# Small matmuls of two heads on two halves of the TensorE array, in fewer and larger groups

## The chip, the core and the metric

The kernel runs on one core of a Trainium2 chip. A core has a 128x128 matmul array (TensorE, in the profile PE, with its weight loads as PEld), VectorE (DVE), ScalarE (ACT), GpSimd (POOL) and SyncE (SP), which here issues the DMAs. Each engine runs its own instructions in order and waits on semaphores for the others. The metric is the device time of one execution in microseconds; lower is better.

## What is computed

One layer of a hybrid decoder on a prompt of 2048 rows and on 8 sequences of 4 new rows, all in fp32, width 1024. The input is normalised and multiplied by one wide matrix. One branch is a short gated convolution, the other an RWKV-7 time mixing with 16 heads of 64; both are projected, gated, added, and projected once more. The part that this change is about is the recurrence of the second branch:

```python
def step(S, inp):
    r_t, k_t, v_t, d_t, kk_t, a_t = inp
    sa = jnp.einsum('bhvk,bhk->bhv', S, -kk_t)
    S = (S * d_t[:, :, None, :] + sa[..., None] * (kk_t * a_t)[:, :, None, :]
         + v_t[..., None] * k_t[:, :, None, :])
    y = jnp.einsum('bhvk,bhk->bhv', S, r_t)
    return S, y
```

S is a 64x64 state per head. It runs over 2048 rows for the prompt and over 4 rows, from a given state, for each of the 8 sequences.

## The kernel before

**Sets, pairs, chunks.** The prompt is cut in 4 sets of 512 rows; the last set carries the 32 sample rows too. The 16 heads go as 8 pairs, one head on partitions 0 to 63 and the other on 64 to 127 (`HS[0]`, `HS[1]`). In each set and pair the recurrence is done in 8 chunks (`NCH`) of 64 rows, so 32 pairs of 8 chunks in all; the samples of a pair are a ninth chunk (index `NCH`) in the last set.

**The steps of a pair** are generators, each a "side":
- `rwkv_keys` makes the scaled keys and queries AR and BK, `[128, chunk, 2, 64]`.
- `rwkv_solve` forms the *scores* (lines 904 to 917): for each chunk and head a matmul of BK by AR over the 64 partitions of that head, four chunks to a group. Head 0 goes to one PSUM tile `pt`, head 1 to another, and DVE masks each into GM. Then it inverts small triangular blocks.
- `rwkv_merge` composes the inverse Xbd with 32x32 matmuls, which are issued head by head in turn (lines 962 to 965).
- `rwkv_load` writes the values of the chunks into `SV[64:128]`.
- `rwkv_chain` (lines 1051 to 1093) runs the chunks in order. Per chunk: a matmul of AR by the state S into `pa`; two DVE additions (one a head) of `pa` and P1 into `us`; `inner`, a matmul of Xbd by `us`, copied into `SV[0:64]` by DVE and ACT; a matmul of BKt by SV; two DVE instructions that make the new S. Those are three links that return to PE: `us`, SV and S.
- `own_values` (1023 to 1032) makes P1 = G K V, what the chunk's own values give: for each chunk and head a 64x64 matmul of GM by `SV[64:128]`, both heads into PSUM partitions 0 to 63, and an ACT copy into P1. It is called for two chunks at a time: once ahead of the chain and three times inside it.
- `own_rows` (1040 to 1049) adds the chunks' own part to the output rows Yc, four chunks to a group: one matmul a chunk with both heads' GM as 128 columns by both heads' SV, which fills four 64x64 blocks of which two are used; two DVE additions pick them. It runs behind the fourth and the eighth chunk.
- `rwkv_sequences` does the same for the samples with w = 1, and `rwkv_out` normalises Yc and stores it.

**What sets the order.** The main stream is projections of 24 passes to a block (`proj`, PSUM tile `ip`), which PE could run without a pause. While the program is built, `drive` goes along the main stream and lets the live sides issue steps between its matmuls. A planner, class `Clock`, keeps a reckoned time of each engine from `Traced.cost`. A side yields the tiles that its next step reads, and is not continued before `clock.t["PE"]` has reached the time at which these are reckoned to be ready, nor before its share of the main stream has come. So the order on each engine is fixed when the program is built, and the costs in `Traced.cost` decide it. The sides of a pair spread over the main stream of a pair; the chain of one pair runs beside keys, solve and merge of the next. Behind the last pair no main stream is left, and what remains of its sides is issued by `finish_sides` (line 1365).

**PSUM.** `pt` has two buffers that all steps but the chain's `pa` and `pb` share.

All instructions are recorded under line 98, the helper, so the profile is read by tile names.

Of the kernel before, what the change touches and what calls it, by code (L numbers as in the profile page):

```python
# [7 lines left out]
F32 = mybir.dt.float32  # L8
# [3 lines left out]
ALU = mybir.AluOpType  # L12
# [4 lines left out]
P = 128  # L17
# [4 lines left out]
NCH = 8  # L22
# [4 lines left out]
W = {"sq": 1.0, "norm": 1.0, "lora": 2.0, "one": 1.0, "scan": 2.0, "exp": 2.0, "key": 1.0, "bones": 1.5,  # L27
     "sv": 1.5, "bt": 2.0, "score": 4.0, "inv0": 5.0, "inv": 0.45, "inv1": 4.0, "merge": 2.0,
     "gk": 1.3, "us": 1.3, "sa": 1.3, "state": 1.3, "samp": 2.0, "gn": 4.0, "out": 2.0}
# [8 lines left out]
class Clock:  # L38
# [3 lines left out]
    def __init__(self):  # L42
        self.t = dict.fromkeys(("PE", "DVE", "ACT", "POOL", "SP"), 0.0)
        self.log = {}
        self.held = {"DVE": [], "POOL": []}

    @staticmethod
# [40 lines left out]
class Traced:  # L88
# [18 lines left out]
    def cost(self, op, out, ins, k):  # L107
        n = out.free_size()
        if self.name == "PE":
            if op == "transpose":  # L110
                return 109.0
            lhs, rhs = k["lhsT"], k["rhs"]
            if rhs.dtype == F32R:
                return 8 + 0.45 * n
            return 2 * max(0.84 * max(lhs.free_size(), n), 26.0)
        if self.name == "DVE":
            per = {"transpose": 1.6, "tensor_tensor_scan": 2.1}.get(op, 1.05)
            if op == "tensor_reduce":
                n = ins[0].free_size()
            return 170 + per * n  # L120
        if self.name == "ACT":
            return 200 + 0.84 * n + 90 * max(0, len(ins) - 1)
        if k.get("op") == ALU.pow:
            return 1650.0
        return 120 + 2.3 * n if op == "tensor_tensor" else 120 + 1.0 * n
# [26 lines left out]
def hybrid_kernel(tc, x_prompt, x_sample, state_conv, state_shift, state_rwkv, norm_g, w_in, conv_w,  # L152
# [220 lines left out]
    rw = ph1.enter_context(tc.tile_pool(name="rw", bufs=1))  # L373
# [15 lines left out]
    SV = xp.tile([P, NC1, P], F32, name="SV")  # L389
# [507 lines left out]
    def rwkv_solve(th, p, o):  # L897

        AR = o["AR"]
        samp = th == LAST  # L900
        GM = GMB[(th * NB + p) % 2]


        for c0 in range(0, NCH + samp, 4):
            cs = range(c0, min(NCH + samp, c0 + 4))
            pp = [ps_t.tile([P, 512], F32, name="pt") for _ in range(2)]
            for h in range(2):
                for c in cs:
                    T.matmul(pp[h][:, (c - c0) * P:(c - c0 + 1) * P], lhsT=BK[HS[h], c].rearrange("p q t -> p (q t)"),
                             rhs=AR[HS[h], c].rearrange("p q t -> p (q t)"), start=True, stop=True)  # L910
            k = len(cs)
            mk = mask_s if c0 == NCH else mask_p
            for h in range(2):
                V.tensor_tensor(out=GM[:, c0:c0 + k, :, h, :],
                                in0=pp[h][:, 0:k * P].rearrange("p (c a t) -> p c a t", a=2, t=64),
                                in1=mk.unsqueeze(1).broadcast_to([P, k, 2, 64]), op=ALU.mult)
            yield W["score"]


        Mc = rw.tile([P, NCH, 32], F32, name="Mc")  # L920
        for i, g in enumerate(blk):
            h, b = i // 2, slice(i % 2 * 32, i % 2 * 32 + 32)
            A.copy(Mc[g], GM[b, 0:NCH, 0, h, b])
        yield 0.5, [Mc]
        Mi = rw.tile([P, 32, 32], F32, name="Mi")
        V.transpose(Mi.rearrange("p t (e c) -> p t e c", c=NCH),
                    Mc.rearrange("p c t -> p t c").unsqueeze(2).broadcast_to([P, 32, 4, NCH]))
        X = rw.tile([P, 8, 32], F32, name="X")
        A.copy(X, X0)
        Mo = rw.tile([P, NCH, 32], F32, name="Mo")  # L930
        A.copy(Mo[64:96], GM[0:32, 0:NCH, 0, 1, 32:64])
        yield W["inv0"], [Mi, X]

        for j in range(31, 0, -1):
            c0 = j // 4
            tt = sm.tile([P, 80], F32, name="tt")
            tv = tt[:, 0:(8 - c0) * j].rearrange("p (c i) -> p c i", i=j)
            V.tensor_tensor(out=tv, in0=Mi[:, j, 0:j].unsqueeze(1).broadcast_to([P, 8 - c0, j]),
                            in1=X[:, c0:8, j:j + 1].broadcast_to([P, 8 - c0, j]), op=ALU.mult)
            V.tensor_tensor(out=X[:, c0:8, 0:j], in0=X[:, c0:8, 0:j], in1=tv, op=ALU.add)  # L940
            yield W["inv"]
        Xo = rw.tile([P, 8, 4, 8], F32, name="Xo")
        V.transpose(Xo.rearrange("p a e c -> p (a e c)"), X.rearrange("p a b -> p (a b)"))
        o.update(GM=GM, Xo=Xo, Mo=Mo)
        yield W["inv"]
# [77 lines left out]
    def own_values(c0, w, GM):  # L1023

        pt = ps_t.tile([P, 512], F32, name="pt")
        for i in range(w):
            for h in range(2):
                T.matmul(pt[0:64, i * P + h * 64:i * P + (h + 1) * 64], lhsT=GM[64:128, c0 + i, 0, h, :],
                         rhs=SV[64:128, c0 + i, HS[h]], start=True, stop=True)
        P1 = sm.tile([64, 2, P], F32, name="P1")  # L1030
        A.copy(P1[:, 0:w, :], pt[0:64, 0:w * P].rearrange("p (c x) -> p c x", x=P))
        return P1

    def inner(c, pb, us, Xbd):

# [4 lines left out]
    def own_rows(c0, w, GM, Yc):  # L1040

        pt = ps_t.tile([P, 512], F32, name="pt")
        for i in range(w):
            T.matmul(pt[:, i * P:(i + 1) * P], lhsT=GM[:, c0 + i, 1].rearrange("p h t -> p (h t)"), rhs=SV[:, c0 + i, :],
                     start=True, stop=True)
        for h in range(2):
            V.tensor_tensor(out=Yc[HS[h], c0:c0 + w, :],
                            in0=pt[HS[h], 0:w * P].rearrange("p (c x) -> p c x", x=P)[:, :, HS[h]],
                            in1=Yc[HS[h], c0:c0 + w, :], op=ALU.add)

    def rwkv_chain(th, p, o):

        Yc = y_tile(th, o)
        AR, pe, GM, Xbd = (o[k] for k in ("AR", "pe", "GM", "Xbd"))
        samp = th == LAST
        S = St[p]

        nxt = own_values(0, 2, GM)
        yield W["gk"], [nxt]
        for g in range(0, NCH, 4):  # L1060
            pa = ps_a.tile([P, 4, P], F32, name="pa")
            for c in range(g, g + 4):
                PC = pe[:, c:c + 1]
                T.matmul(pa[:, c - g, :], lhsT=AR[:, c].rearrange("p q t -> p (q t)"), rhs=S, start=True, stop=True)
                if c % 2 == 0:
                    P1 = nxt
                us = sm.tile([P, 64], F32, name="us")
                for h in range(2):
                    V.tensor_tensor(out=us[HS[h]], in0=pa[0:64, c - g, HS[h]], in1=P1[:, c % 2, HS[h]], op=ALU.add)
                sp = sm.tile([P, P], F32, name="sp")  # L1070
                A.activation(out=sp, in_=S, func=AF.Copy, scale=PC)
                yield W["us"], [us]
                pb = ps_b.tile([P, 2, P], F32, name="pb")
                inner(c, pb[:, 0], us, Xbd)
                yield W["sa"], [SV[0:64, c, :]]
                T.matmul(pb[:, 1, :], lhsT=BKt[:, c, :], rhs=SV[:, c, :], start=True, stop=True)
                for h in range(2):
                    V.scalar_tensor_tensor(out=S[HS[h], HS[h]], in0=pb[HS[h], 1, HS[h]], scalar=PC[HS[h]], in1=sp[HS[h], HS[h]],
                                           op0=ALU.mult, op1=ALU.add)
                if c % 2 == 0 and c + 2 < NCH:  # L1080
                    nxt = own_values(c + 2, 2, GM)
                yield W["state"], [S]
            for h in range(2):
                A.copy(Yc[HS[h], g:g + 4, :], pa[64:128, :, HS[h]])
            yield W["out"], [SV[0:64, g:g + 4]]
            own_rows(g, 4, GM, Yc)
        if samp:
            pt = ps_t.tile([P, 512], F32, name="pt")
            T.transpose(pt[:, 0:P], S, ident)
            so = sm.tile([P, P], F32, name="sq")  # L1090
            V.tensor_copy(so, pt[:, 0:P])
            for h in range(2):
                SP.dma_start(out=new_rwkv_p[0, 0, 2 * p + h], in_=so[HS[h], HS[h]])

    def rwkv_sequences(th, p, o):
# [22 lines left out]
            V.tensor_reduce(out=UY[:, HS[h]], in_=ms.rearrange("p j v -> p v j"), axis=AX.X, op=ALU.add)  # L1118
            A.copy(Yc[HS[h], c, :], UY[64:128, HS[h]])
        us = sm.tile([P, 64], F32, name="us2", bufs=1)  # L1120
        P1 = own_values(c, 1, GM)
        for h in range(2):
            V.tensor_tensor(out=us[HS[h]], in0=UY[0:64, HS[h]], in1=P1[:, 0, HS[h]], op=ALU.add)
        yield W["samp"], [us]
        inner(c, ps_t.tile([P, 512], F32, name="pt"), us, o["Xbd"])
        mss = []
# [364 lines left out]
```

## Time and profile before

| | |
|---|---|
| median of 3 runs | 3385.74 us (3383.95 to 3388.24) |
| the profiled execution | 3391.1 us |
| its span, first to last instruction | 3389.4 us |
| granted TensorE clock, mean | 0.982 |
| instructions | 54068 |
| DMA | 606.60 MB, mean 179 GB/s |

The span is what the profile's windows and timeline run over; the execution takes 1.7 us more. An instruction is written `out<-in`, by tile names without buffer numbers, with rows*columns of the array that a matmul uses: 64*64 is a quarter of it. In the group view the numbers behind the bar are the busy time of the group in us, the mean ns of one, and the idle time of the engine ahead of it with what ended it. In the timeline each row has start and length in us; the end of a matmul record lies some 0.2 us behind the moment at which the array takes the next, so rows overlap, and steps are read from start to start or from end to end.

### The profile page before, as it was taken

What the parts mean: (1) busy time and instruction counts of PE and PEld (TensorE: products, weight loads), DVE (VectorE), ACT (ScalarE), POOL (GpSimd) and SP (SyncE); (2) the same over time, 40 slices, a digit from 0 to 9 for tenths busy, and PEclk for the clock granted to TensorE, in tenths of its full rate; (3) what the DMA queues carried; (4) which work ended last, traced back from release to release, by engine and by line L of the source; (5) the groups of instructions that cost most, each with busy time, mean ns of one, the idle gap of its engine ahead of it and who ended that gap; (6) DMA issues with size and microseconds to landing.
All of it is one profiled execution on the core that took longest, in us unless ns stands there. A gap on an engine that the chain in (4) does not pass through costs nothing.

```text
span 3389.4 us, 54068 instructions
## 1 busy us (share of the span) xinstructions
PE 3257.8 (96%) x20706; PEld 2722.5 (80%) x20706; DVE 2039.6 (60%) x5815; ACT 1265.2 (37%) x2660; POOL 300.2 (9%) x517
## 2 busy tenths in 40 slices
PE   7999999999999999999999999999999997999998
PEld 6777777877777778777777898888888885878897
DVE  5676777766666557555666666677666645433332
ACT  5444444443334443344333344334333332211101
POOL 2110000110001011010001010001000000000000
PEclk9999999999999999999999999999999997999999
DMA  8786666544444444444444443334333347989773
GB/s 278 247 270 209 202 215 214 181 136 137 148 156 146 144 152 167 141 153 140 149 150 150 138 152 116 128 111 135 134 124 105 110 156 243 342 314 324 265 247 130
DMA packets 233305, 606.60 MB, mean 179 GB/s; under 512 B 32906, under 2 KB 136451, under 8 KB 179286
## 3 DMA queue, kind: packets, MB, share of 16 engines
q1 hardware_dynamic: 232902, 602.61, 52.6%
q8 instruction: 164, 2.69, 0.3%
q14 instruction: 95, 0.78, 0.1%
q0 software_dynamic: 144, 0.52, 0.0%
HBM read 447.90 MB, written 155.17 MB: 178 GB/s over the span
## 4 chain that ended last, share of the span: by engine, by line
PE 71%; DVE 16%; issue 5%; ACT 5%; DMA 1%; POOL 1%; DVEq 0%; ACTq 0%; SPq 0%; POOLq 0%
PE ip L98 50%; PE pt L98 12%; PE po L98 5%; DVE X L98 3%; PE pb L98 3%; DVE tt L98 3%; ACT tmp L98 2%; DVE tmp L98 2%; DVE Mi L98 1%; PE pa L98 1%; DVE us L98 1%; DVE whl L98 1%; DVE S L98 1%; ACT Xbd L98 1%; ACT Mc L98 1%
## 5 line engine op out<-in xcount | busy, mean ns | idle before, releaser
L98 PE MATMUL ip<-XH,whl 128*128 128x512 f32 (+3 forms) x7408 | 2053.5, 358 | 6.8 <-ACT whl L98 2.6
L98 PEld LDWEIGHTS ip<-XH,whl 128*128 128x128 f32 x7408 | 1281.9, 191 | 166.8 <-issue 12.8
L98 PE MATMUL ip<-XL,whl 128*128 128x512 f32 (+3 forms) x3704 | 1313.7, 355 | 3.3 <-POOL XL L98 3.3
L98 PEld LDWEIGHTS ip<-XL,whl 128*128 128x128 f32 x3704 | 706.1, 191 | 94.0 <-issue 11.7
L98 DVE TENSOR_TENSOR X<-X,tt 128x60 f32<-128x60 f32 (+24 forms) x992 | 214.5, 216 | 29.4
L98 DVE TENSOR_TENSOR tt<-Mi,X 128x60 f32<-128x60 f32 (+24 forms) x992 | 210.5, 212 | 29.1
L98 DVE SCALAR_TENSOR_TENSOR S<-pb,pe,sp 64x64 f32<-64x64 f32 x512 | 143.4, 280 | 75.9 <-PE pb L98 69.6
L98 ACT COPY SV<-pb 64x64 f32<-64x64 f32 x256 | 53.3, 208 | 362.7 <-DVE SV L98 360.4
L98 PEld LDWEIGHTS pt<-SV,GM 64*64 64x64 f32 (+1 forms) x1584 | 142.5, 155 | 49.1 <-DVE tmp L98 14.5
L98 ACT ACTIVATE tmp<-ip,vec 128x512 f32<-128x512 f32 (+2 forms) x174 | 102.8, 592 | 198.6 <-PE ip L98 196.2
L98 PE MATMUL pt<-SV,GM 64*64 64x64 f32 (+1 forms) x1584 | 167.4, 244 | 9.5 <-DVE tmp L98 7.6
L98 PE MATMUL ip<-RH,whl 128*128 128x512 f32 (+2 forms) x640 | 170.5, 355 | 5.6 <-ACT RH L98 5.6
L98 ACT ACTIVATE sp<-S,pe 128x128 f32<-128x128 f32 x256 | 99.5, 400 | 196.7 <-DVE S L98 194.3
L98 PE MATMUL po<-whl,MH 128*128 128x512 f32 x544 | 170.3, 394 | 0.0
L98 DVE TENSOR_TENSOR us<-pa,P 64x64 f32<-64x64 f32 x512 | 110.6, 216 | 86.3 <-PE pa L98 78.2
L98 DVE TENSOR_TENSOR whl<-wraw,whl 128x1024 fp32r<-128x1024 f32 x105 | 130.2, 1241 | 48.6 <-ACT whl L98 46.6
L98 DVE SCALAR_TENSOR_TENSOR gt<-gt,ip 128x512 f32<-128x512 f32 (+1 forms) x80 | 47.0, 587 | 167.1 <-PE ip L98 164.0
L98 ACT CAST whl<-wraw 128x1024 fp32r<-128x1024 f32 x105 | 109.5, 1043 | 80.4 <-DMA wraw<-in_w_o_dram 20.1
L98 PE MATMUL pt<-AR,BK 64*128 64x128 f32 x1056 | 129.1, 287 | 3.7 <-DVE GM L98 3.7
L98 PEld LDWEIGHTS ip<-RH,whl 128*128 128x128 f32 x640 | 112.7, 189 | 24.6 <-issue 4.0
L98 PEld LDWEIGHTS pb<-us,Xbd 128*128 128x128 f32 x512 | 87.6, 190 | 55.6 <-DVE us L98 18.7
L98 PEld LDWEIGHTS pt<-AR,BK 64*128 64x128 f32 x1056 | 112.2, 188 | 24.6 <-DVE GM L98 8.2
(487 smaller groups left out, 4085.5 us busy)
## 6 DMA issues: line engine op xcount, KB each, us to landing
wraw<-in_w_in_dram SPq DMA_DIRECT2D x81, 512.0 KB
whl<-w_k SPq DMA_DIRECT2D x24, 1024.0 KB
whl<-w_r SPq DMA_DIRECT2D x24, 1024.0 KB
whl<-w_v SPq DMA_DIRECT2D x24, 1024.0 KB
whl<-w_z SPq DMA_DIRECT2D x24, 1024.0 KB
whl<-w_xin SPq DMA_DIRECT2D x24, 1024.0 KB
whl<-w_cg SPq DMA_DIRECT2D x24, 1024.0 KB
whl<-w_zc SPq DMA_DIRECT2D x24, 1024.0 KB
```

The costliest lines, as they stand in the source:

```text
L98: r = f(*a, **k)
```

## The change

Three places issue their matmuls in another way, and the planner reckons narrow matmuls anew.

- Scores: within a group the two heads alternate chunk by chunk, where one head's four came before the other's.
- `own_values`: head 1 writes PSUM partitions 64 to 127, where both wrote 0 to 63, and it is called once for all 8 chunks ahead of the chain. One ACT copy `[128, 512]` makes P1; the calls inside the chain are gone. For the samples DVE reads PSUM directly, with no copy.
- `own_rows`: one matmul a head and chunk, 64 columns wide, head 0 on PSUM partitions 0 to 63 and head 1 on 64 to 127; called once for all 8 chunks behind the chain, with one DVE addition `[128, 512]`.
- `Traced.cost`: an fp32 matmul that uses part of the array costs its time divided by 1.9, and each change of the array's form costs 170 ns.

```diff
+        self.mode = (128, 128)
...
             if rhs.dtype == F32R:
-                return 8 + 0.45 * n
-            return 2 * max(0.84 * max(lhs.free_size(), n), 26.0)
+                mode, t = (P, P), 8 + 0.45 * n
+            else:
+                part = [next(x for x in (32, 64, 128) if v <= x) for v in (lhs.ap[0][1], lhs.free_size())]
+                mode, t = tuple(part), 2 * max(0.84 * max(lhs.free_size(), n), 26.0) / (1 if part == [P, P] else 1.9)
+            t += 170 * (mode != self.clock.mode)
+            self.clock.mode = mode
+            return t
...
-            for h in range(2):
-                for c in cs:
+            for c in cs:
+                for h in range(2):
                     T.matmul(pp[h][:, (c - c0) * P:(c - c0 + 1) * P], lhsT=BK[HS[h], c].rearrange("p q t -> p (q t)"),
                              rhs=AR[HS[h], c].rearrange("p q t -> p (q t)"), start=True, stop=True)
...
         for i in range(w):
             for h in range(2):
-                T.matmul(pt[0:64, i * P + h * 64:i * P + (h + 1) * 64], lhsT=GM[64:128, c0 + i, 0, h, :],
-                         rhs=SV[64:128, c0 + i, HS[h]], start=True, stop=True)
-        P1 = sm.tile([64, 2, P], F32, name="P1")
-        A.copy(P1[:, 0:w, :], pt[0:64, 0:w * P].rearrange("p (c x) -> p c x", x=P))
-        return P1
+                T.matmul(pt[HS[h], i * 64:(i + 1) * 64], lhsT=GM[64:128, c0 + i, 0, h, :], rhs=SV[64:128, c0 + i, HS[h]],
+                         start=True, stop=True)
+        return pt
...
         for i in range(w):
-            T.matmul(pt[:, i * P:(i + 1) * P], lhsT=GM[:, c0 + i, 1].rearrange("p h t -> p (h t)"), rhs=SV[:, c0 + i, :],
-                     start=True, stop=True)
-        for h in range(2):
-            V.tensor_tensor(out=Yc[HS[h], c0:c0 + w, :],
-                            in0=pt[HS[h], 0:w * P].rearrange("p (c x) -> p c x", x=P)[:, :, HS[h]],
-                            in1=Yc[HS[h], c0:c0 + w, :], op=ALU.add)
+            for h in range(2):
+                T.matmul(pt[HS[h], i * 64:(i + 1) * 64], lhsT=GM[:, c0 + i, 1, h, :], rhs=SV[:, c0 + i, HS[h]],
+                         start=True, stop=True)
+        Y = Yc[:, c0:c0 + w, :].rearrange("p c v -> p (c v)")
+        V.tensor_tensor(out=Y, in0=pt[:, 0:w * 64], in1=Y, op=ALU.add)
...
-        nxt = own_values(0, 2, GM)
-        yield W["gk"], [nxt]
+        P1 = rw.tile([P, NCH, 64], F32, name="P1")
+        A.copy(P1.rearrange("p c v -> p (c v)"), own_values(0, NCH, GM))
+        yield W["gk"], [P1]
...
-                if c % 2 == 0:
-                    P1 = nxt
                 us = sm.tile([P, 64], F32, name="us")
                 for h in range(2):
-                    V.tensor_tensor(out=us[HS[h]], in0=pa[0:64, c - g, HS[h]], in1=P1[:, c % 2, HS[h]], op=ALU.add)
+                    V.tensor_tensor(out=us[HS[h]], in0=pa[0:64, c - g, HS[h]], in1=P1[HS[h], c, :], op=ALU.add)
...
-                if c % 2 == 0 and c + 2 < NCH:
-                    nxt = own_values(c + 2, 2, GM)
                 yield W["state"], [S]
...
-            yield W["out"], [SV[0:64, g:g + 4]]
-            own_rows(g, 4, GM, Yc)
+        yield W["out"], [SV[0:64, 0:NCH]]
+        own_rows(0, NCH, GM, Yc)
```

More of the change, by code (lines that the diff above doesn't have):

```diff
@@ L1120, in rwkv_sequences @@
         us = sm.tile([P, 64], F32, name="us2", bufs=1)
-        P1 = own_values(c, 1, GM)
+        pt = own_values(c, 1, GM)
         for h in range(2):
-            V.tensor_tensor(out=us[HS[h]], in0=UY[0:64, HS[h]], in1=P1[:, 0, HS[h]], op=ALU.add)
+            V.tensor_tensor(out=us[HS[h]], in0=UY[0:64, HS[h]], in1=pt[HS[h], 0:64], op=ALU.add)
         yield W["samp"], [us]
```

## The prediction

> **What bounds the kernel now.** I read four views, from coarse to fine. First the page: busy shares, the 40 slices and the chain of work that ended last.
>
> ```profile
> PE 3257.8 (96%) x20706; PEld 2722.5 (80%) x20706; DVE 2039.6 (60%) x5815; ACT 1265.2 (37%) x2660; POOL 300.2 (9%) x517
> PE   7999999999999999999999999999999997999998
> PE 71%; DVE 16%; issue 5%; ACT 5%; DMA 1%; POOL 1%; DVEq 0%; ACTq 0%; SPq 0%; POOLq 0%
> ```
>
> PE is full in all slices but the first, one late and the last, and the chain is mostly PE. A share over the whole span hides stages, so the windows come next: us, then busy us of PE, PEld, DVE, ACT, POOL, clock, DMA share, GB/s.
>
> ```profile
> 84.00:2700.00 2616.00, 2543.90 (x16945) 2122.20 (x16944) 1713.57 (x5133) 1081.55 (x2315) 254.99 (x432) 0.99 0.47 157
> 2780.00:2850.00 70.00, 47.06 (x182) 31.32 (x182) 42.14 (x81) 22.02 (x41) 5.57 (x4) 0.73 0.59 195
> 2850.00:3389.00 539.00, 524.33 (x2608) 441.19 (x2606) 193.74 (x371) 89.43 (x170) 11.43 (x17) 0.99 0.76 273
> ```
>
> In the first row, the stage where all changed code runs, PE is busy 97% and DVE 65.5% (1713.57 of 2616). The second row is the tail of that stage, where one chain of short steps is bare; the third is the merge and output stage, which the change does not touch. What PE waits for, in us, times and the longest, tells what other links are near it:
>
> ```profile
> PE pb L98 <- DVE us L98: 23.0, 37, 1.4
> PE pb L98 <- ACT SV L98: 8.3, 11, 1.6
> PE pa L98 <- DVE S L98: 5.4, 14, 1.0
> ```
>
> The chain's three links cost PE 36.7 us in 62 waits, 0.59 us each. The chain has 32 pairs x 8 chunks x 3 = 768 such links, so 706 pass without one: PE always has projection matmuls to run. Hence a microsecond of PE work taken out of this stage is worth nearly a microsecond of span.
>
> **What the changed matmuls cost now.** Each fp32 matmul is two passes in the trace, so 4 matmuls are "x8". The three groups by form:
>
> ```profile
> L98 PE MATMUL pt<-AR,BK 64*128 64x128 f32 x1056 | 129.1, 287 | 3.7 <-DVE GM L98 3.7
> L98 PE MATMUL pt<-SV,GM 64*64 64x64 f32 x1056 | 94.2, 227 | 8.7 <-DVE tmp L98 7.6 <-ACT tmp L98 1.0
> L98 PE MATMUL pt<-SV,GM 128*128 128x128 f32 x528 | 73.3, 278 | 0.8 <-DVE wraw L98 0.5
> ```
>
> They are scores, own_values and own_rows: 296.6 us that can be cut, an upper limit. Now one own_values group (2 chunks) in the timeline, with its neighbours, and a shorter one:
>
> ```profile
> 1519.89 0.39 PE L98 MATMUL ip<-XH,whl 128*128 128x512 f32 x1
> 1520.22 0.68 PE L98 MATMUL pt<-SV,GM 64*64 64x64 f32 x8
> 1520.82 0.50 PE L98 MATMUL ip<-XH,whl 128*128 128x512 f32 x1
> 1521.16 0.39 PE L98 MATMUL ip<-XL,whl 128*128 128x512 f32 x1
> 1521.39 0.64 PE L98 MATMUL ip<-XH,whl 128*128 128x512 f32 x2
> 1521.86 0.39 PE L98 MATMUL ip<-XL,whl 128*128 128x512 f32 x1
> ...
> 1557.34 0.44 PE L98 MATMUL pt<-SV,GM 64*64 64x64 f32 x4
> ```
>
> From ip XL to ip XL are three passes in 0.70 us: a normal step is 0.23. The ip before the group ends at 1520.28, the one behind at 1521.32; less one step the group takes **0.81 us**. Four passes more lengthen the row from 0.44 to 0.68, so one pass is 0.06 and eight are 0.48. The other 0.33 is the change of array form from 128*128 to 64*64 and back: the group begins only when the ip before it is nearly out, and the ip behind has 0.50 where others have 0.39.
>
> Scores and own_rows, likewise:
>
> ```profile
> 1549.48 2.01 PE L98 MATMUL pt<-AR,BK 64*128 64x128 f32 x16
> 1551.41 0.50 PE L98 MATMUL ip<-XH,whl 128*128 128x512 f32 x1
> 1551.75 1.05 PE L98 MATMUL pt<-SV,GM 128*128 128x128 f32 x8
> ...
> 1553.80 0.39 PE L98 MATMUL ip<-XH,whl 128*128 128x512 f32 x1
> 1554.12 1.71 PE L98 MATMUL pt<-AR,BK 64*128 64x128 f32 x16
> 1555.75 0.50 PE L98 MATMUL ip<-XH,whl 128*128 128x512 f32 x1
> ```
>
> own_rows has no change of form: it ends at 1552.80, the ip before it at 1551.91, so **0.89 us** for 8 passes, 0.11 each. The second scores group takes 1556.25 - 1554.19 - 0.23 = **1.83 us**, 0.12 beyond its row; the first, with the same overhead, 2.13. Sixteen passes in series are 1.76 plus 0.33 = 2.09: the first ran in series, the second overlapped the two heads for two or three passes.
>
> **Do two tiles of the array run at once?** The gain hangs on this, and the kernel has both kinds:
>
> ```profile
> 1509.52 0.21 PE L98 MATMUL pt<-T,GM 32*32 32x32 f32 x1
> 1509.52 0.21 PE L98 MATMUL pt<-T,Mo 32*32 32x32 f32 x1
> 1509.57 0.19 PE L98 MATMUL pt<-T,GM 32*32 32x32 f32 x1
> 1509.58 0.19 PE L98 MATMUL pt<-T,Mo 32*32 32x32 f32 x1
> ...
> 2512.70 1.08 PE L98 MATMUL pt<-tmp,BKt 128*64 128x512 f32 x4
> ```
>
> The first four are issued head by head in turn, as the change does: both heads start together, on other rows and columns of the array. The last is the case of column halves on the same rows: two matmuls of 512 columns, four passes. At 0.11 us for 128 columns a pass is 0.44, four in series 1.76; the row is 1.08, so the halves ran side by side.
>
> The Trainium skill, page "TensorE: Matmul & The Clock Gate", section Part 3 on packing small matmuls, speaks against the change: a weight load overlaps a running matmul only where the row group differs, and column halves share theirs. By that rule own_values and own_rows would gain nothing from halves, the second rival below; the row of 1.08 disagrees.
>
> **The change part by part.**
>
> *own_values*: 4 groups a pair become one of 16 matmuls, 32 passes in 16 slots of two: 16 x 0.06 + 0.33 = 1.29. Per pair 4 x 0.81 - 1.29 = 1.95; times 32 pairs **62 us**.
>
> *Scores*: 64 groups. Alternated, 16 passes fill 8 slots of 0.11: 0.88 + 0.33 = 1.21. Saved 0.62 (from the 1.83 kind) to 0.92 (from 2.13), 40 to 59 us for all; the 1.83 kind is the nearer to steady running, and alternation may have to wait for the second PSUM buffer one matmul in, not four: I take **42 us**, and 37 as the low end.
>
> *own_rows*: two groups of 0.89 become one in 128*64 form. It now pays the change of form: 16 x 0.06 + 0.33 = 1.29 (the slot from own_values, since weights and moving are 64 columns in both). 1.78 - 1.29 = 0.49 a pair, **16 us**. No row has 64 columns in this form: bounds are 0.89, as now (28 us), and 32 passes in series, 2.25 (a loss of 15).
>
> *Samples* (8 pairs of the last set): own_values saves 0.12, scores 0.22, own_rows loses 0.23, each a few passes; under 1 us, nothing.
>
> *Evacuations* beside PE:
>
> ```profile
> L98 DVE TENSOR_TENSOR Yc<-pt,Yc 64x256 f32<-64x256 f32 x128 | 53.8, 420 | 31.4 <-PE pt L98 30.1
> L98 ACT COPY P<-pt 64x256 f32<-64x256 f32 x128 | 46.6, 364 | 84.6 <-PE pt L98 82.1 <-DVE us L98 1.5
> 1549.58 0.69 DVE L98 TENSOR_TENSOR bv<-pt,vT 128x512 f32<-128x512 f32 x1 [1.51 <-PE pt L98]
> 1530.84 0.57 ACT L98 COPY tmp<-ip 128x512 f32<-128x512 f32 x1
> ```
>
> DVE's four additions of 0.42 a pair become one of about 0.69, ACT's four copies of 0.364 one of about 0.57: 1.0 and 0.9 us less a pair, under the cover of PE. I count them as nothing. The additions that form `us` keep their shape and count.
>
> *New waits*: the chain's first `us` waits for 1.29 + 0.57 where it was 0.81 + 0.36, 0.7 us later a pair; queued behind it on DVE is work of other sides, and PE meanwhile runs projections. Without that cover it is 32 x 0.7 = 22 us. own_rows of chunks 0 to 3 moves behind the second four chunks; that place already held a group, and who reads Yc starts behind the whole chain. No DMA, SP or POOL instruction moves.
>
> *The planner*: its PE time decides where sides are issued. It reckoned an own_values group at 4 x 107 ns = 0.43 us, against 0.81 run; the new formula gives 16 x 107.5 / 1.9 + 340 ns = 1.25 for the new one, close to 1.29. Every other narrow matmul is reckoned anew too, so the whole order shifts. I bound that by nothing and by twice the present 36.7 us of chain waits, and take 10 us lost, the low part, since the cover stays.
>
> **Sum**: 62 + 42 + 16 - 10 = 110 us. The profiled execution took 3391.1 (span 3389.4 and 1.7 around it), which gives 3281; the median of the runs is 5.4 lower, 3385.7, and gives **3276**. Its own range is 3256 to 3300: scores at 59 and no loss, or scores at 37 and 30 lost.
>
> **The rivals.**
>
> 1. *Freed PE time becomes waits.* With less PE work per pair the same DVE work fills more of it; if the chain's waits double, 37 us more go, and the time is 3313. For it: 62 waits stand there today, the last set among them, with shorter projections. Against: DVE at 65.5%, and the evacuations shrink.
> 2. *Column halves take turns.* own_values is then 32 x 0.06 + 0.33 = 2.25 a pair, saving 32 us; own_rows loses 15; scores keep 42; less 10, 3337. Against: the row of 1.08. For: no row has 64-column passes on halves, where loads count more.
> 3. *It does not do what it says*: alternated matmuls run in order too. Scores then cost 2.09 where the two kinds average 1.98, 7 us worse; with 32 - 15 - 10 the sum is nothing, 3386. Against: the rows at 1509.52.
> 4. *Slower: the re-planned order issues chain steps too early.* Place: the head of PE's queue, where a matmul waiting for `us`, SV or S holds all projections behind it. Price 0.59 us a link. It eats the 120 us of gains when 203 more links of the 768 wait; 350 more give 206, and 3472. Against: today 62 do, and the planner still sees the same DVE and ACT durations.
>
> **How the numbers follow.** About 0.2% (7 us) is what a measurement of this kernel can tell from no change. Forecast 0.67; a still larger gain, below 3256, 0.05; rival 1, 0.14; rival 2, 0.06; rival 3, 0.03; rival 4, 0.05. Faster is 0.67 + 0.05 + 0.14 + 0.06 = 0.92, same 0.03, slower 0.05. The range 3256 to 3322 holds the forecast and most of rival 1, 0.8; rivals 2 to 4 lie above it.
>
> **What would show it.** In the profile after: own_values as one row of 32 passes of about 1.16 us (2.1 if the halves take turns), 64*64, once a pair; scores x16 rows of about 1.1 (1.7 to 2.0 if not); own_rows on 128*64, x32, about 1.16; chain waits of PE near 37 us (rival 1: near 74; rival 4: over 150); busy PE in the stage falling with the span, the merge and output stage unchanged at 539. Wrong would be a span that falls by less than half of what these rows lose: then the order, not the array, has become the bound.

## The result

The changed kernel takes 3308.55 us (median of 4 runs, 3304.68 to 3311.7), the kernel before 3386.99 in the same comparison: a ratio of 0.9769, 95% interval 0.9752 to 0.9786, or 78 us less. The forecast was 3276 in a range of 3256 to 3322. The direction is right and the time lies in the range, but 110 us had been reckoned, 32 more than came.

The page of the changed kernel, the lines that were read first:

```profile
PE 3178.0 (96%) x21234; PEld 2641.5 (80%) x21234; DVE 2010.1 (61%) x5711; ACT 1244.2 (38%) x2556; POOL 307.3 (9%) x517
PE   7999999999999999999999999999999988999998
PE 71%; DVE 16%; issue 5%; ACT 5%; DMA 2%; POOL 1%; DVEq 0%; SPq 0%; ACTq 0%; POOLq 0%
```

Shares and chain are as they were: PE is still the bound and lost 79.8 us of busy time (3257.8 to 3178.0), about what the span lost (3389.4 to 3308.9). The stages, from the windows of the changed kernel with the same columns as before:

```profile
84.00:2620.00 2536.00, 2466.96 (x17500) 2046.65 (x17499) 1693.02 (x5050) 1063.11 (x2220) 262.29 (x432) 0.99 0.49 162
2699.00:2769.00 70.00, 45.82 (x170) 29.41 (x169) 37.89 (x72) 19.02 (x35) 5.58 (x4) 0.68 0.54 180
2769.00:3308.00 539.00, 524.64 (x2609) 441.29 (x2607) 193.62 (x371) 89.73 (x170) 11.46 (x17) 0.99 0.76 273
```

The main stage is 80 us shorter at the same 97% of PE; merge and output are as before. So the question is what PE runs in that stage. The three groups by form, in the changed kernel:

```profile
L99 PE MATMUL pt<-AR,BK 64*128 64x128 f32 x1056 | 116.7, 287 | 1.0 <-DVE GM L99 0.9
L99 PE MATMUL pt<-SV,GM 128*64 128x64 f32 x1056 | 44.7, 228 | 3.7 <-DVE wraw L99 1.9 <-DVE SV L99 1.6
L99 PE MATMUL pt<-SV,GM 64*64 64x64 f32 x1056 | 39.9, 223 | 4.7 <-DVE tmp L99 4.7
```

Scores are busy 116.7 where it was 129.1, own_rows 44.7 (73.3), own_values 39.9 (94.2). Busy time leaves out the changes of form. So each group of the trace was also taken as in the prediction, from the end of the pass ahead to the end of the pass behind, less a normal step of that pass, idle time included, and summed (the sums move by 1 to 3 us with the step that is taken as normal):

| PE's time, us | before | after | change | forecast |
|---|---|---|---|---|
| own_values | 126.8 | 53.7 | -73.1 | -62 |
| scores | 142.6 | 128.0 | -14.6 | -42 |
| own_rows | 73.4 | 65.6 | -7.8 | -16 |
| everything else | | | +15.0 | +10 |
| span of the profiled execution | 3389.4 | 3308.9 | -80.5 | -110 |

The row "everything else" is the rest that makes up the span. Scores are 27 us of the 30 that are missing, own_rows 8, the rest 5, and own_values gave 11 more than reckoned.

**The array did what was forecast.** The timeline of the changed kernel, start and length in us: an own_values group, an own_rows group with what follows, and the two scores groups of one pair.

```profile
155.84 1.15 PE L99 MATMUL pt<-SV,GM 64*64 64x64 f32 x32
156.91 0.50 PE L99 MATMUL ip<-XL,whl 128*128 128x512 f32 x1
...
997.68 1.15 PE L99 MATMUL pt<-SV,GM 128*64 128x64 f32 x32
998.76 0.65 PE L99 MATMUL pt<-ident,vT 128*128 128x128 f32 x4
...
1046.27 2.01 PE L99 MATMUL pt<-AR,BK 64*128 64x128 f32 x16
1048.21 0.50 PE L99 MATMUL ip<-XL,whl 128*128 128x512 f32 x1
1048.54 0.38 PE L99 MATMUL pb<-SV,BKt 128*128 128x128 f32 x2
1048.68 0.48 PE L99 MATMUL ip<-XH,whl 128*128 128x512 f32 x1
1049.09 1.16 PE L99 MATMUL pt<-AR,BK 64*128 64x128 f32 x16
```

Thirty-two passes in 1.15 us, both with 64*64 and with 128*64: 1.16 had been forecast, and the column halves run side by side. The second scores group takes 1.16, near the 1.1 forecast. The first takes 2.01, exactly as before the change. It runs in series although the source alternates the heads. The built program tells why; this is its own order on PE for these two groups (x3: three more of the same):

```
pt_10536 x4
pt_10537 [waits DVE]
pt_10537 x3
...
pt_10553 [waits DVE]
pt_10554 [waits DVE]
pt_10553
pt_10554
```

Head 1's PSUM tile `pt_10537` still waits for DVE to empty it. The build puts each engine's instructions in the order in which it reckons them ready, so it moved head 0's four matmuls ahead. Counted over the program, 242 of 447 neighbouring score matmuls are still of the same head, where it was 382 of 459. The trace agrees: of the 41 rows x16 of scores 19 take about 1.16 us, the others 1.5 and more.

### The profile page after: what moved, and what is told of

Read it like the earlier page. It is cut to its first block, busy times and chain, and to the rows that moved or that the text cites. A ratio compares the mean times of both kernels' runs of the same rounds, so it can differ in the third digit from the quotient of the medians.

```text
span 3308.9 us, 54886 instructions
## 1 busy us (share of the span) xinstructions
PE 3178.0 (96%) x21234; PEld 2641.5 (80%) x21234; DVE 2010.1 (61%) x5711; ACT 1244.2 (38%) x2556; POOL 307.3 (9%) x517
## 3 DMA queue, kind: packets, MB, share of 16 engines
q1 hardware_dynamic: 232902, 602.61, 53.7%
## 4 chain that ended last, share of the span: by engine, by line
PE 71%; DVE 16%; issue 5%; ACT 5%; DMA 2%; POOL 1%; DVEq 0%; SPq 0%; ACTq 0%; POOLq 0%
PE ip L99 50%; PE pt L99 11%; PE po L99 6%; PE pb L99 3%; ACT tmp L99 3%; DVE tt L99 3%; DVE X L99 2%; DVE tmp L99 2%; DVE Mi L99 1%; PE pa L99 1%; DVE S L99 1%; DVE us L99 1%; DVE whl L99 1%; DVE AR L99 1%; DVE GM L99 1%
## 5 line engine op out<-in xcount | busy, mean ns | idle before, releaser
L99 ACT COPY SV<-pb 64x64 f32<-64x64 f32 x256 | 53.7, 210 | 261.4 <-DVE SV L99 258.6
L99 PEld LDWEIGHTS pb<-SV,BKt 128*128 128x128 f32 x512 | 86.6, 190 | 52.6 <-ACT SV L99 41.3
L99 PE MATMUL pb<-SV,BKt 128*128 128x128 f32 x512 | 107.3, 291 | 18.6 <-ACT SV L99 17.3
L99 PEld LDWEIGHTS po<-whl,MH 128*128 128x128 f32 x544 | 102.2, 188 | 23.7
L99 PE MATMUL pt<-AR,BK 64*128 64x128 f32 x1056 | 116.7, 287 | 1.0 <-DVE GM L99 0.9
```

The lines of the kernel that those rows point to most:

```text
L99: r = f(*a, **k)
```

## The experiments

The theory was that the missing time is this order of the scores, because `pt` has two buffers; the rival, that the scores gave what was forecast and waits took it back. Times in different comparisons are set side by side through the ratio to the kernel before.

**scores_by_head.** The alternation undone.

```diff
-            for c in cs:
-                for h in range(2):
+            for h in range(2):
+                for c in cs:
```

> The changed kernel with the scores issued head by head again. Theory: the missing part of the gain is the scores. The build puts PE's instructions in the order in which it reckons them ready, and in the changed kernel's program 242 of 447 neighbouring score matmuls are still of the same head (382 of 459 in the kernel before), so the scores gave 15 us where 42 were forecast; undone, they cost 12 to 20 us and the time is 3320 to 3329. Rival: the scores gave their 42 and the loss is in waits of the chain; then 3345 to 3355.

3336.81 us, ratio 0.9856 (0.9838 to 0.9874): 29 us slower than the changed kernel, between the two expectations and in neither. PE's time for the scores rose only from 128.0 to 140.9. More than half of the loss is elsewhere, and the waits of PE show where:

```profile
PE pb L99 <- DVE us L99: 25.3, 40, 1.9
```

That link is 14.7 us in the changed kernel; all idle time of PE rises from 115.6 to 129.7. So undoing the alternation costs 13 us of PE's time for the scores and 14 of waits. That the scores, ending later, shift what stands ahead of the chain's links is the likely reason; no run shows it apart.

**scores_touch.** The alternation enforced.

```diff
+            both = [V.memset(t[0:1, 0:1], 0.0) for t in pp]
             for c in cs:
                 for h in range(2):
-                    T.matmul(pp[h]...)
+                    r = T.matmul(pp[h]...)
+                    if (c, h) == (c0, 0):
+                        tc.add_manual_dep(r.ins, both[1].ins.name, Sync)
+                    else:
+                        tc.keep_in_program_order(r)
```

> The changed kernel with the scores' alternation enforced: DVE writes one element of both PSUM tiles of a group first, the group's first matmul waits for that, and each further one stays behind the one before it. All 456 neighbours alternate in the program. Theory: 64 groups of 1.25 us take 80 where the changed kernel's take 128; less some waiting, 25 to 45 us gained, 3264 to 3284. Rival (two row halves do not run together for whole groups, or the PSUM tiles' evacuation sets the pace): within 8 us of 3308.

3338.92 us, ratio 0.9854 (0.9839 to 0.987): a miss of both. The array did its part: the scores' time fell from 128.0 to 88.6, near the 80 of 64 full groups of 1.25. Yet the kernel is 29 us slower than the changed one. The scores by form, the writes, and a wait of PE that is nearly new (1.9 us in the kernel before):

```profile
L99 PE MATMUL pt<-AR,BK 64*128 64x128 f32 x1056 | 78.3, 286 | 0.7 <-DVE pt L99 0.4 <-DVE ncv L99 0.3
...
L99 DVE MEMSET pt<- 1x1 f32 x144 | 8.2, 59 | 0.7 <-ACT SV L99 0.3
...
PE pt L99 <- DVE T L99: 19.0, 25, 1.8
```

The writes are cheap in themselves. PE idles 151.9 us in all where it was 115.6, which is 36 of the 68 us between gain and loss. The likely reason is that the groups, made to wait for both tiles, come later, and with them what depends on them; the wait for T fits that, but no run separates it. The rest, 32 us, lies in PE's steps. The granted clock is 0.975, where the changed kernel has 0.982: the share that was not granted makes 83 us of 3339.2 here and 60 of 3308.9 there, so up to 24 of the 32 can be the clock (an estimate, as if PE had had work in all of that time).

**three_pt.** A third buffer for `pt`, taken from `pa`.

```diff
-    ps_t = ph1.enter_context(tc.tile_pool(name="ps_t", bufs=2, space=PSUM))
-    ps_a = ph1.enter_context(tc.tile_pool(name="ps_a", bufs=2, space=PSUM))
+    ps_t = ph1.enter_context(tc.tile_pool(name="ps_t", bufs=3, space=PSUM))
+    ps_a = ph1.enter_context(tc.tile_pool(name="ps_a", bufs=1, space=PSUM))
```

> The changed kernel with three buffers of the PSUM tile pt instead of two, and one of pa instead of two; nothing pinned. 369 of 457 neighbouring score matmuls alternate in the program. Theory: the order of the scores is spoilt by the second PSUM tile of a group coming free late; with a third buffer 15 to 30 us are gained, 3279 to 3294, unless the chain waits for its one pa buffer. Rival: no gain, 3300 to 3315.

3264.41 us, ratio 0.9637 (0.9619 to 0.9654): 45 us faster than the changed kernel, more than expected. By form, the scores:

```profile
L99 PE MATMUL pt<-AR,BK 64*128 64x128 f32 x1056 | 95.1, 288 | 1.4 <-DVE us L99 0.6
```

With the form changes they take 105.7 where the changed kernel has 128.0. That is 37 below the kernel before, so the forecast 42 is nearly there once the second PSUM tile is free. But 22 us of passes do not make 45. Another place where two matmuls stand on the two row halves, each with a `pt` of its own, gains too: the low-rank matmuls (`lora`, `up`) in `rwkv_keys`. The same place in the changed kernel and in three_pt:

```profile
393.73 1.12 PE L99 MATMUL pt<-lora,up 64*128 64x512 f32 x2
395.02 1.12 PE L99 MATMUL pt<-lora,up 64*128 64x512 f32 x2 [0.17 <-DVE ss L99]
```

```profile
388.37 1.13 PE L99 MATMUL pt<-lora,up 64*128 64x512 f32 x4
```

With two buffers the second matmul waits until DVE has emptied a `pt` into `ss`, and starts 1.3 us behind the first; with three both are done in the time of one. In both forms together (64x512 and 64x32) these matmuls are busy 56.5 us in the changed kernel and 45.1 here, and the idle time ahead of own_values, 4.7 us there, is nothing here. With the scores that makes 38 of the 45. The chain's waits rise in spite of it, from 41.3 to 47.5 us; whether that is the one `pa` buffer was not tested.

**three_by_head and before_three** complete the square of order and buffers: three_pt with the loops of scores_by_head, and the kernel before with the two lines of three_pt.

> Three buffers of pt and one of pa, as in three_pt (3264 us), but the scores issued head by head: 86 of 462 neighbouring score matmuls alternate in the program, 369 of 457 in three_pt. Theory: what three_pt gained over the changed kernel is mostly the order of the scores that the third buffer allows; without it the passes of the scores take 30 us more and the chain's waits some, 3290 to 3310. Rival: the third buffer gains by itself (two heads' low-rank matmuls side by side, fewer waits); then within 10 us of 3264.

> The kernel before with three buffers of pt and one of pa, nothing else. Theory: its scores are head by head in any case (96 of 478 neighbours alternate), so a third buffer gains only the low-rank matmuls' 8 us of passes and some waits: 3360 to 3380. Rival: the buffer alone is worth the 44 us that three_pt gained over the changed kernel; then 3335 to 3350.

3289.25 us, ratio 0.9713 (0.9697 to 0.973), just under the theory's span; and 3347.34, ratio 0.9886 (0.9871 to 0.9901), the rival's span.

| ratio to the kernel before | pt x2 | pt x3 |
|---|---|---|
| kernel before | 1 | 0.9886 |
| changed, scores head by head | 0.9856 | 0.9713 |
| changed | 0.9769 | 0.9637 |

Down the columns the alternation is worth 0.0087 with two buffers and 0.0076 with three, 29 and 26 us. Along the rows the third buffer is worth 39, 48 and 45 us, with or without alternation. So what three_pt gained over the changed kernel is not mostly the order that the third buffer allows, as the theory had it: the buffer is worth as much head by head (48 us) as alternated (45), and the alternation no more with three buffers than with two. Head by head, the scores took 120.8 us with three buffers and 140.9 with two: with a free tile the second head's passes begin beside the first's even in the old order, as in the 1.71 us group of the prediction. In the trace of three_by_head no row x16 of scores takes 2.0 us or more, in that of scores_by_head 12 of 32 do. The low-rank matmuls, which the rival named, are busy 45.0 us there, 53.8 in scores_by_head.

**old_planner.** The changed kernel with the two old lines of `Traced.cost`.

> The changed kernel with the planner's old costs in Traced.cost: the same matmuls, reckoned without the division by 1.9 and without the 170 ns for a change of form. Theory: the planner's new numbers are a small part, as forecast (10 us either way), 3298 to 3320; the program's scores alternate about as often (226 of 443 neighbours). Rival: the new costs are what keeps the chain's waits low; then over 3325.

3301.62 us, ratio 0.975 (0.9735 to 0.9764), not slower than with the new costs; the intervals overlap. The new costs are no source of the gain.

**rows_pinned.** own_rows in one run.

```diff
-        for i in range(w):
+        for i in reversed(range(w)):
             for h in range(2):
-                T.matmul(pt[HS[h], i * 64:(i + 1) * 64], ...)
+                r = T.matmul(pt[HS[h], i * 64:(i + 1) * 64], ...)
+                if (i, h) != (w - 1, 0):
+                    tc.keep_in_program_order(r)
```

> The changed kernel with own_rows issued from the last chunk to the first, each matmul kept behind the one before it, so that a group is one run on PE. Theory: in the tail of the last pair the 16 matmuls of own_rows stand as 16 separate pieces between the chain's links, each with a change of the array's form, and the pair took 71.2 us where it took 66.1 before; in one run 4 to 7 us come back, 3301 to 3305. Rival: those pieces stand where PE is idle anyway; no change, or 1 us slower, since the rows then start later.

The 71.2 and 66.1 us there run from the end of the last SV matmul of the pair before to that of the last pair. The tail of the changed kernel, in the timeline:

```profile
2679.43 0.33 PE L99 MATMUL pt<-SV,GM 128*64 128x64 f32 x2 [0.31 <-DVE SV L99]
2679.68 0.49 PE L99 MATMUL pb<-SV,BKt 128*128 128x128 f32 x2
2680.10 0.33 PE L99 MATMUL pt<-SV,GM 128*64 128x64 f32 x2
```

Pieces of own_rows, 128*64, stand between the chain's links, which are 128*128, so that each link follows a change of form. With the pieces in one run, the timeline of rows_pinned shows one group:

```profile
2706.08 1.97 PE L99 MATMUL pt<-SV,GM 128*64 128x64 f32 x30
```

3303.03 us, ratio 0.9752 (0.9738 to 0.9767). The time is where the theory put it, but the intervals overlap; the trace is clearer: own_rows fall from 65.6 to 55.7, 17.7 below the kernel before, where 16 had been forecast, and the last pair takes 66.9 us (2639.3 to 2706.2) where the changed kernel takes 71.2.

**values_by_two.** Column halves kept, the grouping undone.

```diff
-        A.copy(P1.rearrange("p c v -> p (c v)"), own_values(0, NCH, GM))
+        def two(c0):
+            A.copy(P1[:, c0:c0 + 2, :].rearrange("p c v -> p (c v)"), own_values(c0, 2, GM)[:, 0:2 * 64])
+        two(0)
...
+                if c % 2 == 0 and c + 2 < NCH:
+                    two(c + 2)
                 yield W["state"], [S]
```

> The changed kernel with own_values on the two column halves, but for two chunks at a time again: one call ahead of the chain and three inside it. Reckoned by slots it is 4 x (4 x 0.06 + 0.33) = 2.28 us a pair where one group takes 1.29, 32 us more. Theory: groups inside the chain also stood where PE waits for SV (that link cost PE 8.3 us before and 17.3 in the changed kernel, and its weight loads 20.8 and 41.3), so part comes back: 10 to 24 us slower than the changed kernel, 3318 to 3332. Rival: the place does not matter, or the smaller groups take the pt buffers from the scores more often; 28 to 45 us slower, 3336 to 3353.

3315.17 us, ratio 0.979 (0.9774 to 0.9806): 7 us above the changed kernel, with overlapping intervals, and below the theory's span. own_values take 96.0 us of PE where the group of 8 takes 53.7, 42 more, yet the kernel is hardly slower. The waits of PE, first of the changed kernel, then of this one:

```profile
PE pb L99 <- ACT SV L99: 17.3, 26, 2.4
PE pb L99 <- DVE us L99: 14.7, 24, 1.8
PE pa L99 <- DVE S L99: 9.3, 22, 1.0
```

```profile
PE pb L99 <- DVE us L99: 8.4, 18, 1.2
PE pb L99 <- ACT SV L99: 6.8, 11, 1.5
PE pa L99 <- DVE S L99: 3.7, 9, 0.7
```

41.3 us of chain waits against 18.9: the small groups inside the chain go with shorter waits. The run also makes the first part of P1 ready sooner, but that can weigh only on the first chunk's `us`, where PE's waits are 8.3 us in the changed kernel and 2.5 here, 6 of the 22. Place is not all, though: the kernel before has its groups in the chain too, and waits 36.7. The weight loads of the SV link, from the group views of the kernel before and of the changed one, wait longer as well:

```profile
L98 PEld LDWEIGHTS pb<-SV,BKt 128*128 128x128 f32 x512 | 87.5, 190 | 34.0 <-ACT SV L98 20.8
```

```profile
L99 PEld LDWEIGHTS pb<-SV,BKt 128*128 128x128 f32 x512 | 86.6, 190 | 52.6 <-ACT SV L99 41.3
```

**three_rows, three_rows_old, three_rows_scores, three_all_old**: what gained, together. The first is three_pt with rows_pinned; the second adds the old planner's costs; the third adds to three_rows the line `tc.keep_in_program_order` on every score matmul of a group but its first; the fourth has all.

> three_pt with own_rows from the last chunk to the first in one run, as in rows_pinned. Theory: the two gains are in different places, scores in every pair and own_rows in the tail of the last pair, and add up: 3264 less 4 to 7, 3257 to 3260. Rival: with three buffers the tail no longer suffers from the pieces; 3262 to 3268.

> three_rows (3262 us) with the planner's old costs. old_planner came out 7 us below the changed kernel, so the new costs may lose a little. Theory: they do, through the waits of the chain, and 3 to 10 us are gained: 3252 to 3259. Rival: that was a shift in the order that does not carry over; 3258 to 3270.

> three_rows with each score matmul kept behind the one before it in its group, with no wait added: 438 neighbours alternate and none is of the same head (369 and 88 in three_rows), but the group's first matmul can stand alone, and the scores make 90 separate runs on PE where they made 71. Theory: 10 us of passes are saved and 19 more runs cost 0.33 us each, 6: 3255 to 3262. Rival: the pinned order makes PE wait for the second buffer, as with the writes of scores_touch; 3265 to 3285.

> Everything that gained, together: the changed kernel with three buffers of pt and one of pa, own_rows in one run from the last chunk, each score matmul behind the one before it, and the planner's old costs. Theory: the steps add up, 3250 less the 8 us that the pinned scores gave: 3238 to 3246. Rival: pinned scores and old costs shift the same waits and do not add: 3247 to 3256.

| | us | ratio, 95% interval |
|---|---|---|
| three_rows | 3261.74 | 0.9632 (0.9618 to 0.9647) |
| three_rows_old | 3249.79 | 0.9598 (0.9584 to 0.9612) |
| three_rows_scores | 3253.26 | 0.9608 (0.9594 to 0.9622) |
| three_all_old | 3253.62 | 0.9602 (0.9589 to 0.9615) |

three_rows is between its two expectations, and its interval overlaps that of three_pt. The old costs gain 12 us here, 2 more than expected at most; pinned scores 8, a little more than expected, with intervals that just overlap; both together, in the rival's span, no more than either. The best is three_rows_old, 4% below the kernel before and 1.8% below the changed one (0.9598 / 0.9769).

## Why the prediction was right, and where it was too large

**The range.** Its low end was added up wrong: scores at 59 and no loss make 62 + 59 + 16 = 137 us and 3249, not 3256. The measured time is at the other end, so nothing hangs on it.

**The bound** was right: PE was full, and the span fell by what PE's busy time fell.

**Slots and form changes** were right. own_values and own_rows run 32 passes in 1.15 us on halves, so rival 2, halves in turns, is out; a scores group whose heads alternate takes 1.16.

**Scores is the step that failed**, 42 us forecast and 14.6 found. It took the order in the source for the order on PE. The prediction did write that alternation may have to wait for the second PSUM buffer, but priced that as a late start, 37 instead of 42. What happened is that the build issued one head's four matmuls while the other tile was not free, and that half of the neighbours never alternated. scores_touch, where all neighbours alternate and the buffers are still two, brings PE's time for the scores to 88.6, -54 us against the kernel before; three_pt, with 369 of 457 alternating, to -37, and three_rows_scores, with 438 and none of the same head, to 101.5, -41. So the array can give the forecast 42; how much of it is left in the kernel's time is another matter, as scores_touch shows.

**own_rows** was right as a group and too large in all: in the tail of the last pair its matmuls stood one by one. rows_pinned gives -17.7.

**own_values** gave 11 us more than its term. Some of its old groups had been split, each piece with its own change of form (the rows x4 of the prediction): in the trace of before, 136 groups make 150 runs on PE, some 5 us at 0.33 each. The idle time ahead of them also fell, from 8.7 to 4.7 us. But "the cover stays" does not hold for the whole: of 42 us that grouping saves on PE, as values_by_two shows, some 22 come back in chain waits (41.3 against 18.9), some 11 in PE's own steps at the three links (203 us against 192, from end to end without idle time), and 7 are left in time. The price that the prediction put on a later first `us`, 22 us without cover, did not come: PE's waits there went from 5.9 to 8.3 us. Of the +15 where +10 had been taken, 12 lie at the chain's links: 4.6 of waits and 7.7 in PE's steps there (195.6 us before, 203.3 after). That the groups taken out of the chain had covered it is the likeliest reason; it was not shown apart from the new order.

**The planner's 10 us** lost was of the right size: 0.0019 of the ratio, 6 us, in the changed kernel (not clear of noise), 12 in three_rows. That the new costs match the array better did not make a better order.

Rival 1, waits in place of work, came at about an eighth of its price: chain waits are 41.3 us where they were 36.7, 4.6 more of the 37 that it gave. Rival 3 came for half of the scores, by another way: not the array but the built order kept them in series. Rival 4 did not come.

The third buffer is worth 39 us to the kernel before (43 between the two profiled executions). The traces place most of it: 26.7 in the scores (142.6 to 115.9), 8.7 in the low-rank matmuls and the idle time ahead of them, 7.9 in the idle time ahead of own_values, against 7.5 more of chain waits (36.7 to 44.2). What stays open: the remaining 7 us there, why values_by_two waits less for its chain than the kernel before, and what divides the loss of scores_touch.

## What to carry to other kernels

Small matmuls on different halves of the array paid here only where they stood beside each other in the engine's own queue, and that took a free PSUM buffer for both outputs when the first one was placed: read the built order, not the source. Grouping saves the changes of the array's form, but a group that is taken out of a chain of dependent steps may have been what covered the chain's waits; count it on both sides. Where many steps share two PSUM buffers, try a third before changing the steps: here, at the price of one `pa` buffer, it gained 39 to 48 us in each of the three kernels that it was tried on, half or more of what the whole change gave.

## What the runs showed of the hardware that was not expected

Two 64-column matmuls on the column halves run as well side by side with 128 rows as with 64, 1.15 us for 32 passes each. A scores group in which every matmul alternates needs no more than the slots of one head, 1.16 us against 2.01, even with all 128 columns loaded for each pass. And a buffer that comes free late costs in more places than the one that was looked at: two low-rank matmuls of 512 columns on the row halves took 1.13 us in all with a buffer each, and twice 1.12, one after the other, where the second had to wait for its buffer.
